# Issuing the low-half matmuls of a split-precision product after all the high-half ones

## The chip, the cores and the metric

The kernel runs on one core of a Trainium2 chip. The metric is device time of one execution in microseconds (us). The five engines of the core work from queues of their own: TensorE (matmuls, in the profile PE, with its weight loads as PEld), VectorE (DVE), ScalarE (ACT), GpSimd (POOL) and SyncE (SP, here only an issuer of transfers). They wait for one another by semaphores.

## The reference, cut to what matters

A residual stream of 16 meta tokens and 512 tokens of width 1024 goes through two layers. Layer 0 mixes by causal pooling, layer 1 by an attention over keys and values that are projected once. Each layer then has a PEER block: every token picks 8 x 16 of 16384 experts by two sets of 128 sub-keys, and adds their outputs.

```
def peer(h, w_query, sub_keys, u, v):
    q = einsum('btd,dq->btq', hx, w_query)            # query projection
    s = einsum('bthpc,hpnc->bthpn', q, sub_keys)      # scores of the sub-keys
    top_s, top_i = lax.top_k(s, 16)
    ...                                               # 256 sums, top 16, softmax -> expert, gate
    act = gelu(einsum('btd,bthkd->bthk', hx, u[expert]))
    return einsum('bthk,bthkd->btd', gate * act, v[expert])
```

## The kernel before, in words

Of the four blocks of 128 tokens three are treated densely: for each of the 128 groups of 128 experts the kernel forms gelu(u . h) for all 384 tokens (a "first product", function `u_parts`, called a step here), weighs it with a gate matrix that is zero where an expert was not picked, and multiplies by v. The experts of the fourth block (`GATHERED`) are fetched row by row with indirect transfers (`row_steps`: `prod` L354, `hx` L366 on VectorE, `row` L342 on GpSimd).

Products are of float32 values split into two halves: hi is the value rounded to the format that TensorE reads at full rate, lo is the rest. A product is hi*hi + hi*lo + lo*hi over 8 chunks of 128 in depth, 24 matmuls into one PSUM bank. In a step the weights are the stationary operand: `w_hi` (copied from the loaded `w32` by ScalarE, L278) and `w_lo` (w minus w_hi, on VectorE L280 while `gating` is set, otherwise on GpSimd L282). Both have two buffers, `w32` has three, and `load_w` of a step is called one step ahead (`following`). The moving operand is the normalised stream, `n_hi` and `n_lo`.

A PEER block has three stages. In the query stage 16 projections (two per head) and their scores alternate with steps; layer 0's projections have two PSUM tiles because of the meta tokens (L516, L517), layer 1's go through `mm3` (L123 to L125, here with weights stationary). The scores' matmuls (L530) feed VectorE's top-16 searches (`top16`, `tv`). In the gate stage `select` picks the experts on VectorE, and `build_gates` forms one-hot tiles (`hot` L612, `weighed` L616) for 8 tokens at a time, 16 such groups in each of 3 blocks, which TensorE multiplies into `pg` (L596) in groups of 16 matmuls; ScalarE copies `pg` to `stage`, which goes to memory as `gout`. Steps are cut into quarters at a `yield` (`UPARTS` = 4), and a hand-written cost account (`tu`, `td`) decides after which quarters of steps the `pg` groups stand. While `pinned` is set, TensorE's matmuls keep this order; the other queues, and TensorE's outside this stage, are ordered when the program is built, by a planner that follows program order among what its own estimate holds to be ready. In the value stage the remaining steps alternate with `v_step` (matmuls `y`, L713), whose weights `v` come straight from memory.

`mm3` is also used in the attention: for the projections to keys, queries and values (`pp` with `wn_hi`, `wn_lo`) and for its output projection (`wo_hi`, `wo_lo`). There the stream is stationary and the weights move: `whi` is `n_hi` and `wlo` is `n_lo`.

Of the kernel before, what the change touches and what calls it, by code (L numbers as in the profile page):

```python
# [22 lines left out]
KC = D // P  # L23
# [15 lines left out]
UPARTS = 4  # L39
# [19 lines left out]
def trunk_kernel(ctx: ExitStack, tc: tile.TileContext, x, meta, norm_mix, norm_ffn, pool_w, pool_scale,  # L59
                 kv_norm, w_kv, k_norm, w_q, q_norm, w_o, peer_wq, peer_keys, peer_ut, peer_uv, out):  # L60
    nc = tc.nc
    v, sc, pe, gp, sy = nc.vector, nc.scalar, nc.tensor, nc.gpsimd, nc.sync
# [58 lines left out]
    def mm3(ps, whi, wlo, xhi, xlo, kc):  # L121
        for k in range(kc):
            pe.matmul(ps, whi(k), xhi(k), start=k == 0, stop=False)  # L123
            pe.matmul(ps, whi(k), xlo(k), start=False, stop=False)  # L124
            last = pe.matmul(ps, wlo(k), xhi(k), start=False, stop=k == kc - 1)  # L125
        return last

# [126 lines left out]
    def peer(layer, with_meta, gain, hn_nat, kp, up, finish):  # L254
# [3 lines left out]
        c0 = dense[0] * P  # L258
        assert dense == list(range(dense[0], dense[0] + nd))
        ND = nd * P  # L260
# [3 lines left out]
        SM = S + NM if with_meta else S  # L264
        hi, lo = n_hi, n_lo

        with ExitStack() as cl:
# [3 lines left out]
            vmark, amark, pmark, todo = [], [], [], []  # L271
# [17 lines left out]
            def pin(x):  # L289
                return tc.keep_in_program_order(x) if pinned[0] else x  # L290
# [8 lines left out]
            def weight(key, following=None):  # L299
# [3 lines left out]
                        ahead[kk] = load_w(src[layer, kk[1]])  # L303
                return ahead.pop(key)

            def u_parts(j, spill, following=None):
                w, whi, wlo = weight(("u", j), following)
                ps = psu.tile([P, S], F32, name="psu")
                n = 0
                for k in range(KC):  # L310
                    for a, b, st, en in ((whi, hi, k == 0, False), (whi, lo, False, False),
                                         (wlo, hi, False, k == KC - 1)):
                        m = pin(pe.matmul(ps[:, :ND], a[:, k, :], b[:, k, c0:c0 + ND], start=st, stop=en))  # L313
                        n += 1
                        if n == 3 * KC:
                            pmark.append(m)
                        elif n * UPARTS % (3 * KC) == 0:
                            yield
                ac = up.tile([P, ND], F32, name="ac", bufs=FRONT + 2)
                sc.activation(ac, ps[:, :ND], AF.Gelu)  # L320
                if spill:
                    sc.dma_start(aout[j], ac)
                return ac
# [57 lines left out]
            with ExitStack() as c1:  # L381
# [92 lines left out]
                with ExitStack() as cq:  # L474
                    qp = cq.enter_context(tc.tile_pool(name="qp", bufs=1, reuse_waits="tile"))
                    keys = qp.tile([P, 2 * H, NK], F32, name="keys")
                    sy.dma_start(keys, peer_keys[layer])
                    if with_meta:
                        zq = qp.tile([P, 2 * H, H, NM], F32, name="zq")
                        psq = cq.enter_context(tc.tile_pool(name="psq", bufs=2, reuse_waits="tile", space=PSUM))  # L480
                        gp.memset(zq, 0.0)
                    plan = []
                    nu = 0
                    for _ in range(LEAD[layer]):
                        plan.append(("u", nu))
                        nu += 1
                    for h in range(H):
                        plan += [("w", 2 * h), ("w", 2 * h + 1)]
                        td += WQ_DVE[layer]
                        tu += WQ_PE[layer]  # L490
                        while tu < td and h > 0:
                            plan.append(("u", nu))
                            nu += 1
                            tu += ucost
                    plan.append(("u", nu))
                    plan.reverse()
                    while plan[-1][0] == "u":
                        u_step(plan.pop()[1], True, plan[-1])
                        j0 += 1
                    norm_split(gr, ps1, NT - 1, hx[NT - 1], gain, hn_nat[NT - 1], pt_name="ps1", junk="prod")  # L500
                    ym = kp.tile([P, D], F32, name="gain") if with_meta else None

                    for h in range(H):
                        qts = []
                        for pp in range(2):
                            hp = 2 * h + pp
                            w, whi, wlo = weight(plan.pop(), plan[-1])
                            ps = psu.tile([P, S], F32, name="psu")
                            qt = qp.tile([P, S], F32, name="qt", bufs=3)
                            if with_meta:  # L510
                                half = SM // 2
                                ps2 = psq.tile([P, half], F32, name="psq")
                                for k in range(KC):
                                    for wp, xp, st, en in ((whi, hi, k == 0, False), (whi, lo, False, False),
                                                           (wlo, hi, False, k == KC - 1)):
                                        pe.matmul(ps[:, :half], wp[:, k, :], xp[:, k, :half], start=st, stop=en)  # L516
                                        pe.matmul(ps2, wp[:, k, :], xp[:, k, half:SM], start=st, stop=en)  # L517
                                sc.activation(qt[:, :half], ps[:, :half], AF.Copy)
                                sc.activation(qt[:, half:], ps2[:, :S - half], AF.Copy)
                                sc.activation(zq[:, hp, h, :], ps2[:, S - half:], AF.Copy)  # L520
                            else:
                                mm3(ps, lambda k: whi[:, k, :], lambda k: wlo[:, k, :],
                                    lambda k: hi[:, k, :S], lambda k: lo[:, k, :S], KC)
                                sc.activation(qt, ps, AF.Copy)
                            qts.append(qt)
                        for i2 in range(0, NT, 2):
                            pss = ps1.tile([P, 2, 2, NK], F32, name="ps1")
                            for ii in range(2):
                                for pp in range(2):
                                    pe.matmul(pss[:, ii, pp, :], qts[pp][:, (i2 + ii) * P:(i2 + ii + 1) * P],  # L530
                                              keys[:, 2 * h + pp, :], start=True, stop=True)
                            s = qp.tile([P, 2, 2, NK], F32, name="s", bufs=3)
                            sc.activation(s, pss, AF.Copy)
                            for ii in range(2):
                                for pp in range(2):
                                    top16(qp, s[:, ii, pp, :], NK, tv[i2 + ii][:, h, pp, :],
                                          ti[i2 + ii][:, h, pp, :])
                        tq += 26.0 if h >= GH else 0.0
                        while len(plan) > 1 and plan[-1][0] == "u":
                            u_step(plan.pop()[1], True, plan[-1])  # L540
                            j0 += 1
                        if h % GH == GH - 1:
                            hs = slice(h - GH + 1, h + 1)
                            for i in gathered:
                                res = []
                                for _ in select(qp, gr, f"g{i}_{h}", tv[i][:, hs], ti[i][:, hs], GH, res):
                                    pass
                                gather_rows(i, h, *res, GH * TK, hx[i], False)
                        while tr < tq and row_step():
                            tr += ROW_PERIOD[layer][0] / 8  # L550
                    if with_meta:
                        pss = ps1.tile([P, 2, 2, NK], F32, name="ps1")
                        for pp in range(2):
                            for h in range(H):
                                pe.matmul(pss[:, 0, pp, :], zq[:, 2 * h + pp].rearrange("p g t -> p (g t)"),
                                          keys[:, 2 * h + pp, :], start=h == 0, stop=h == H - 1)
                        s = qp.tile([P, 2, 2, NK], F32, name="s", bufs=3)
                        sc.activation(s[:, 0], pss[:, 0], AF.Copy)
                        for pp in range(2):
                            top16(qp, s[:, 0, pp, :], NK, tvm[:, 0, pp, :], tim[:, 0, pp, :])  # L560
# [515 lines left out]
```

## Time and profile before

| | us |
|---|---|
| median of 3 runs | 3077.86 |
| lowest and highest of them | 3077.44, 3078.27 |
| the profiled execution | 3071.0 |
| its span, first to last instruction | 3069.3 |
| TensorE busy in the span | 2914.3 (95%) |
| TensorE weight loads busy | 2597.2 (85%) |
| VectorE busy | 2321.5 (76%) |
| ScalarE busy | 1313.3 (43%) |
| GpSimd busy | 664.3 (22%) |

The profile is one execution. A group of instructions is told with its busy time and the idle time of its engine just before it, by whom that wait was ended. A line of the chain of waits is a piece of the work that ended last, followed back from the end. Where an engine is named as the one waited for, its instruction was the last of several conditions to come true by the profile. Idle time of an engine that does not set the end of a stretch costs nothing.

### The profile page before, as it was taken

How to read it: one execution, taken by the hardware profiler on the slowest of the kernel's cores; microseconds unless marked ns; L12 is line 12 of the kernel's file. 1: busy time of each engine (PE TensorE's matmuls, PEld its weight loads, DVE VectorE, ACT ScalarE, POOL GpSimd, SP SyncE). 2: the span in 40 equal slices, each digit the busy share in tenths (PEclk: the TensorE clock that was granted, in tenths of full speed). 3: DMA queues.
4: the chain of work that ended last, by engine and by line, in shares of the span. 5: the costliest groups of instructions: out<-in, count | busy, mean ns of one | idle time of the engine just before them, and what ended most of it. 6: DMA issues, size and time to landing. Idle time of an engine off the chain costs nothing.

```text
span 3069.3 us, 45150 instructions
## 1 busy us (share of the span) xinstructions
PE 2914.3 (95%) x16514; PEld 2597.2 (85%) x16514; DVE 2321.5 (76%) x4807; ACT 1313.3 (43%) x2154; POOL 664.3 (22%) x702
## 2 busy tenths in 40 slices
PE   8987999999999999999999998798999999999999
PEld 7977898988888887779965787798998888888887
DVE  3699979678887878866456437999777888788875
ACT  3323646454333333344456333355546333333333
POOL 3441111111211211104235244311110211111100
PEclk9998999999999999999999999999999999999999
DMA  3266778789999999952100324677887999898985
GB/s 131 99 234 217 267 271 314 268 329 392 325 341 325 337 316 328 366 187 80 56 1 1 110 100 172 231 248 278 285 306 284 364 350 334 310 338 312 377 278 168
DMA packets 294768, 769.50 MB, mean 251 GB/s; under 512 B 24080, under 2 KB 184848, under 8 KB 256400
## 3 DMA queue, kind: packets, MB, share of 16 engines
q1 hardware_dynamic: 226576, 396.43, 38.0%
q0 software_dynamic: 39168, 285.23, 24.8%
q10 hardware_dynamic: 28800, 84.95, 7.2%
q8 instruction: 129, 2.11, 0.3%
q14 instruction: 95, 0.78, 0.1%
HBM read 679.49 MB, written 87.03 MB: 250 GB/s over the span
## 4 chain that ended last, share of the span: by engine, by line
PE 76%; DVE 15%; DMA 5%; ACT 2%; issue 2%; POOL 1%; SPq 0%; DVEq 0%; ACTq 0%; POOLq 0%
PE y L713 30%; PE psu L313 27%; DMA v<-in_peer_uv_dram 3%; PE pp L124 2%; PE pp L125 2%; PE pp L123 2%; PE pg L596 2%; DVE w_lo L280 2%; DVE prod L354 1%; PE psq L517 1%; PE psu L516 1%; DVE hx L366 1%; DVE weighed L616 1%; DVE hot L612 1%; DVE mr L394 1%
## 5 line engine op out<-in xcount | busy, mean ns | idle before, releaser
L313 PE MATMUL psu<-n_hi,w_lo 128*128 128x384 f32 x2048 | 700.2, 342 | 73.7 <-DVE w_lo L280 69.4
L342 POOL DMA_INDIRECT row<-in_peer_uv_dram,ei x272 | 363.8, 1337 | 1767.5 <-DVE hx L366 1492.2
L313 PE MATMUL psu<-n_hi,w_hi 128*128 128x384 f32 x2048 | 707.6, 346 | 4.4 <-ACT w_hi L278 3.9
L313 PE MATMUL psu<-n_lo,w_hi 128*128 128x384 f32 x2048 | 699.9, 342 | 0.6 <-DVE n_lo L118 0.6
L278 ACT ACTIVATE w_hi<-w 128x1024 fp32r<-128x1024 f32 x288 | 305.2, 1061 | 498.2 <-PE psu L313 351.0
L713 PE MATMUL y<-v_hi,wt_hi 128*128 128x512 f32 x1536 | 474.9, 390 | 6.5 <-ACT wt_hi L705 4.5
L713 PE MATMUL y<-v_lo,wt_hi 128*128 128x512 f32 x1536 | 475.8, 391 | 5.1 <-DVE v_lo L699 5.0
L713 PE MATMUL y<-v_hi,wt_lo 128*128 128x512 f32 x1536 | 474.6, 390 | 1.2 <-DVE wt_lo L706 1.2
L313 PEld LDWEIGHTS psu<-n_hi,w_lo 128*128 128x128 f32 x2048 | 391.5, 191 | 82.9 <-DVE w_lo L280 77.1
L313 PEld LDWEIGHTS psu<-n_hi,w_hi 128*128 128x128 f32 x2048 | 389.2, 190 | 9.1 <-ACT w_hi L278 5.2
L313 PEld LDWEIGHTS psu<-n_lo,w_hi 128*128 128x128 f32 x2048 | 389.9, 190 | 3.9 <-DVE n_lo L118 1.1
L705 ACT ACTIVATE wt_hi<-wt 128x384 fp32r<-128x384 f32 x256 | 134.3, 525 | 529.5 <-PE y L713 292.7
L280 DVE TENSOR_TENSOR w_lo<-w,w_hi 128x1024 fp32r<-128x1024 f32 x230 | 280.1, 1219 | 100.0 <-ACT w_hi L278 98.9
L713 PEld LDWEIGHTS y<-v_lo,wt_hi 128*128 128x128 f32 x1536 | 288.1, 188 | 69.4 <-DVE v_lo L699 10.1
L713 PEld LDWEIGHTS y<-v_hi,wt_lo 128*128 128x128 f32 x1536 | 289.0, 188 | 62.3 <-DVE wt_lo L706 2.0
L354 DVE SCALAR_TENSOR_TENSOR prod<-row,hnat 128x1024 bf16<-128x1024 f32 x272 | 337.9, 1242 | 5.0 <-DMA row<-in_peer_uv_dram,ei 4.8
L713 PEld LDWEIGHTS y<-v_hi,wt_hi 128*128 128x128 f32 x1536 | 288.0, 188 | 62.8 <-ACT wt_hi L705 5.0
L366 DVE SCALAR_TENSOR_TENSOR hx<-row,gwt,hx 128x1024 f32<-128x1024 f32 x256 | 329.6, 1287 | 2.6
L699 DVE TENSOR_TENSOR v_lo<-v,v_hi 128x1024 fp32r<-128x1024 f32 x256 | 312.1, 1219 | 20.2 <-ACT v_hi L698 20.2
L698 ACT ACTIVATE v_hi<-v 128x1024 fp32r<-128x1024 f32 x256 | 270.9, 1058 | 61.0 <-DMA v<-in_peer_uv_dram 59.3
L706 DVE TENSOR_TENSOR wt_lo<-wt,wt_hi 128x384 fp32r<-128x384 f32 x256 | 142.1, 555 | 203.2 <-ACT wt_hi L705 202.9
L601 ACT ACTIVATE stage<-pg 128x512 f32<-128x512 f32 x192 | 200.9, 1156 | 81.7 <-PE pg L596 80.9
(283 smaller groups left out, 4110.6 us busy)
## 6 DMA issues: line engine op xcount, KB each, us to landing
w<-in_peer_ut_dram SPq DMA_DIRECT2D x256, 512.0 KB, 5.2
v<-in_peer_uv_dram SPq DMA_DIRECT2D x256, 512.0 KB, 6.8
gout<-stage ACTq DMA_DIRECT2D x24, 2048.0 KB, 8.4
gt<-gout SPq DMA_DIRECT2D x64, 768.0 KB, 9.8
aout<-ac ACTq DMA_DIRECT2D x176, 192.0 KB, 3.5
ac<-aout SPq DMA_DIRECT2D x176, 192.0 KB, 7.0
w<-in_peer_wq_dram SPq DMA_DIRECT2D x32, 512.0 KB, 3.3
wn<-in_w_kv_dram SPq DMA_DIRECT2D x8, 1024.0 KB, 5.5
```

The source lines that it names most:

```text
L278: amark.append(sc.activation(whi, w, AF.Copy))
L280: vmark.append(v.tensor_sub(wlo, w, whi.bitcast(F32)))
L313: m = pin(pe.matmul(ps[:, :ND], a[:, k, :], b[:, k, c0:c0 + ND], start=st, stop=en))
L342: gp.indirect_dma_start(out=row, out_offset=None, in_=peer_uv, in_offset=bass.IndirectOffsetOnAxis(ap=item[1], axis=0))
L354: v.scalar_tensor_tensor(prod, row[:, :D], 1.0, hn_nat[i], ALU.mult, ALU.mult, accum_out=dot)
L366: v.scalar_tensor_tensor(acc, row[:, D:], wt, acc, ALU.mult, ALU.add)
L601: sc.activation(stage[:, :, o:o + 4].rearrange("p j t -> p t j"), pg, AF.Copy, scale=1.0 / GSCALE)
L698: amark.append(sc.activation(vhi, v32, AF.Copy))
L699: vmark.append(v.tensor_sub(vlo, v32, vhi.bitcast(F32)))
L705: sc.activation(whi, wt, AF.Copy)
L706: vmark.append(v.tensor_sub(wlo, wt, whi.bitcast(F32)))
L713: pe.matmul(y[n][half], wp[:, ts], vq[:, half * 512:(half + 1) * 512], start=st, stop=en)
```

## The change

For each product over 8 chunks the order of the 24 matmuls is changed. Before: for each chunk k, `w_hi[k]` with the stream's high half, `w_hi[k]` with its low half, `w_lo[k]` with its high half. After it: for all chunks the two products with `w_hi`, then for all chunks the product with `w_lo`. This holds for the steps, for layer 0's projections (each of the 24 there is a pair of matmuls), and for everything that calls `mm3`. The sums, the number of matmuls, the buffers and the places of the yields by count of matmuls stay as they are.

```diff
@@ -122,6 +122,7 @@
         for k in range(kc):
             pe.matmul(ps, whi(k), xhi(k), start=k == 0, stop=False)
             pe.matmul(ps, whi(k), xlo(k), start=False, stop=False)
+        for k in range(kc):
             last = pe.matmul(ps, wlo(k), xhi(k), start=False, stop=k == kc - 1)
         return last
@@ -303,19 +304,25 @@
+            def low_last(whi, wlo):
+
+                for k in range(KC):
+                    yield whi, hi, k, k == 0, False
+                    yield whi, lo, k, False, False
+                for k in range(KC):
+                    yield wlo, hi, k, False, k == KC - 1
+
             def u_parts(j, spill, following=None):
                 w, whi, wlo = weight(("u", j), following)
                 ps = psu.tile([P, S], F32, name="psu")
                 n = 0
-                for k in range(KC):
-                    for a, b, st, en in ((whi, hi, k == 0, False), (whi, lo, False, False),
-                                         (wlo, hi, False, k == KC - 1)):
-                        m = pin(pe.matmul(ps[:, :ND], a[:, k, :], b[:, k, c0:c0 + ND], start=st, stop=en))
-                        n += 1
-                        if n == 3 * KC:
-                            pmark.append(m)
-                        elif n * UPARTS % (3 * KC) == 0:
-                            yield
+                for a, b, k, st, en in low_last(whi, wlo):
+                    m = pin(pe.matmul(ps[:, :ND], a[:, k, :], b[:, k, c0:c0 + ND], start=st, stop=en))
+                    n += 1
+                    if n == 3 * KC:
+                        pmark.append(m)
+                    elif n * UPARTS % (3 * KC) == 0:
+                        yield
@@ -510,11 +517,9 @@
-                                for k in range(KC):
-                                    for wp, xp, st, en in ((whi, hi, k == 0, False), (whi, lo, False, False),
-                                                           (wlo, hi, False, k == KC - 1)):
-                                        pe.matmul(ps[:, :half], wp[:, k, :], xp[:, k, :half], start=st, stop=en)
-                                        pe.matmul(ps2, wp[:, k, :], xp[:, k, half:SM], start=st, stop=en)
+                                for wp, xp, k, st, en in low_last(whi, wlo):
+                                    pe.matmul(ps[:, :half], wp[:, k, :], xp[:, k, :half], start=st, stop=en)
+                                    pe.matmul(ps2, wp[:, k, :], xp[:, k, half:SM], start=st, stop=en)
```

## Rows read from the trace of the kernel before

**Rows 1.** The page: span, engines, one of its costliest groups (busy, mean ns | idle before).
```profile
span 3069.3 us, 45150 instructions
...
PE 2914.3 (95%) x16514; PEld 2597.2 (85%) x16514; DVE 2321.5 (76%) x4807; ACT 1313.3 (43%) x2154; POOL 664.3 (22%) x702
...
L313 PE MATMUL psu<-n_hi,w_lo 128*128 128x384 f32 x2048 | 700.2, 342 | 73.7 <-DVE w_lo L280 69.4
```

**Rows 2.** Busy times by stretch: us, PE, PEld, DVE, ACT, POOL, PEclk, DMA share, GB/s.
```profile
143.00:217.00 74.00, 60.07 (x445) 58.56 (x444) 69.62 (x297) 24.12 (x53) 36.29 (x20) 0.91 0.58 213
219.40:410.80 191.40, 158.30 (x1039) 152.85 (x1037) 186.14 (x598) 95.95 (x133) 32.50 (x17) 0.91 0.68 242
410.80:648.00 237.20, 231.00 (x1634) 224.11 (x1635) 190.30 (x237) 132.32 (x177) 26.33 (x19) 0.99 0.80 291
...
672.00:1186.00 514.00, 512.57 (x2463) 451.16 (x2461) 422.83 (x614) 196.67 (x330) 94.90 (x79) 1.00 0.94 340
...
1947.50:2126.30 178.80, 148.65 (x956) 142.34 (x954) 174.48 (x534) 88.70 (x124) 32.03 (x18) 0.93 0.69 248
2126.30:2362.00 235.70, 230.40 (x1612) 223.66 (x1613) 188.77 (x234) 130.21 (x173) 28.35 (x18) 0.99 0.82 292
```

**Rows 3.** TensorE's waits (us, times, longest), gate stages' halves: two of the first, then one each.
```profile
PE psu L313 <- DVE w_lo L280: 31.4, 7, 19.3
PE pg L596 <- DVE weighed L616: 1.7, 1, 1.7
...
PE psu L313 <- DVE w_lo L280: 4.8, 4, 2.3
...
PE psu L313 <- DVE w_lo L280: 27.6, 8, 9.2
...
PE psu L313 <- DVE w_lo L280: 6.5, 5, 2.3
```

**Rows 4.** VectorE's waits: layer 0's first half (two), its second, layer 1's first (two).
```profile
DVE hot L612 <- PE pg L596: 4.4, 2, 2.3
DVE w_lo L280 <- ACT w_hi L278: 0.7, 2, 0.4
...
DVE w_lo L280 <- ACT w_hi L278: 34.9, 21, 3.0
...
DVE w_lo L280 <- ACT w_hi L278: 2.6, 3, 1.5
DVE hot L612 <- PE pg L596: 1.0, 1, 1.0
```

**Rows 5.** The chain of waits (start, us, what): a value-stage step, a gate-stage step.
```profile
681.76 4.23 PE psu L313 x24
...
2174.63 4.29 PE psu L313 x24
```

**Rows 6.** The chain of waits after a wait for `w_lo`, layer 0's first half.
```profile
340.73 3.57 PE psu L313 x10
344.30 1.73 PE pg L596 x16
```

**Rows 7.** TensorE's waits from 217 to 219.4 us, at layer 0's gate entry.
```profile
PE psu L313 <- POOL w_lo L282: 2.2, 1, 2.2
```

**Rows 8.** Layer 1's query stage, 1866 to 1947 us: waits, one piece of the chain.
```profile
PE psu L125 <- POOL w_lo L282: 9.2, 2, 6.1
...
DVE tv L392 <- ACT s L533: 9.6, 1, 9.6
...
1903.30 0.23 PE psu L124
```

**Rows 9.** Groups by line: the attention's projections with the weights' low half.
```profile
L124 PE MATMUL pp<-wn_lo,n_hi 128*128 128x256 f32 x384 | 109.9, 286 | 0.0
...
L124 PE MATMUL pp<-wo_lo,n_hi 128*128 128x256 f32 x128 | 37.2, 292 | 1.7 <-DVE wo_lo L1006 1.7
```

**Rows 10.** The chain of waits at the end of layer 0's gate stage.
```profile
649.90 11.21 DMA gout<-stage
```

## The prediction

> **What bounds the kernel now.** I read the page first: one span of 3069.3 us [rows 1] in an execution of 3071.0 us, 6.9 us under the median of the three timed runs (3077.86 us); differences are formed on the profiled execution and then taken off the median. Its costliest groups show the target: the matmuls of a first product that read the low half `w_lo` stood behind 73.7 us of idle TensorE, nearly all of it waiting for VectorE's subtraction at L280 [rows 1]. That adds up stages with different limits, so the busy times by stage come next. In the value stage TensorE is busy 512.6 of 514 us: nothing can be hidden there. The gate stages have two halves. In the first half of each (219.4 to 410.8 us in layer 0, 1947.5 to 2126.3 us in layer 1) VectorE is busy 186.1 of 191.4 and 174.5 of 178.8 us, TensorE only 158.3 and 148.7; in the second half TensorE is busy 231.0 of 237.2 and 230.4 of 235.7 us and VectorE has room [rows 2]. So the first halves belong to VectorE, the second halves to TensorE.
>
> The waits say how the lost time divides. TensorE waits for `w_lo` 31.4 and 27.6 us in the first halves, but 4.8 and 6.5 us in the second [rows 3]. VectorE in turn idles in the first halves only 4.4 and 1.0 us for `pg` matmuls that free a `hot` buffer, and 0.7 and 2.6 us for a `w_hi` that waits for its own buffer; in layer 0's second half the latter is 34.9 us, which is its room [rows 4]. A wait of TensorE in a stretch that VectorE fills costs the end nothing; VectorE's own idle time there does.
>
> **The change part by part.** It adds and removes no instruction: a step has the same 24 matmuls and weight loads, 3 products for 8 chunks. It moves eight of them behind sixteen.
>
> (a) The head start. Before, `w_lo` is read by the third matmul of a step, after it by the seventeenth. A step of 24 matmuls of 384 columns takes 4.23 us [rows 5], 0.176 us each, so `w_lo` may come 14 x 0.176 = 2.46 us later before anything stands. For layer 1's projections of 512 columns a matmul takes 0.23 us [rows 8], so there it is 14 x 0.23 = 3.2 us. The quarters end after 6, 12 and 18 matmuls as before; a gate group `pg` that follows matmul 12 now stands ahead of the wait for `w_lo` and no longer behind it.
>
> (b) The early release. The last read of `w_hi` was matmul 23 and becomes matmul 16: 7 x 0.176 = 1.2 us earlier for the ScalarE copy L278 that refills it, and so for VectorE's next subtraction. `w_lo` is released at matmul 24 as before. The load of the next `w32` on SP waits for a subtraction, so no transfer is moved later on its queue, at most 1.2 us earlier.
>
> The sum, stretch by stretch:
> 1. Entry of layer 0's gate stage: TensorE stands 2.2 us for a `w_lo` from GpSimd [rows 7], in its order ahead of the score matmuls that VectorE then waits for. 2.2 is under 2.46: 2.2 us.
> 2. First half, layer 0: VectorE's idle 4.4 + 0.7 us. The chain shows its making: TensorE resumes after a `w_lo` wait, needs 3.57 us for 10 matmuls and 1.73 us for the 16 of `pg`, and only then may `hot` be built [rows 6]. With (a) that `pg` precedes the wait; with (b) the `w_hi` waits, 0.4 us at most each, go. 5.1 us.
> 3. Second half, layer 0: four waits, the longest 2.3 us, all under 2.46: 4.8 us.
> 4. First half, layer 1: VectorE's 1.0 + 2.6 us, for the same reasons: 3.6 us.
> 5. Second half, layer 1: five waits, the longest 2.3 us: 6.5 us.
> 6. Query stage, layer 1: L125 waits twice for GpSimd's `w_lo`, 6.1 and 3.1 us, and VectorE then stands 9.6 us for scores that come out of that stretch [rows 8]. Of the 6.1 us the head start takes 3.2; the 3.1 I count at nothing, because VectorE is busy when they pass (if it weren't, they would be 3.1 us more). In layer 0's query stage VectorE is busy 69.6 of the last 74 us [rows 2], so TensorE's waits there count nothing.
>
> 2.2 + 5.1 + 4.8 + 3.6 + 6.5 + 3.2 = 25.4 us.
>
> What it could cost. Pace: in the low run the weights go from one `w_lo` chunk to the next, an order that the trace does not show. The same 24 matmuls took 4.23 us in the value stage and 4.29 in a gate stage [rows 5]. I take 4.23, the row where TensorE is disturbed least; the upper end is 0.06 x 256 steps = 15 us. A gain is excluded: no matmul, column or load disappears. The projections through `mm3` in the attention are mirrored: there the weights are the moving operand, and chunk k is now needed after 2k matmuls and not 3k, at most 7 matmuls earlier, which are shorter than L313's, so under 7 x 0.176 = 1.2 us. TensorE waited 0.0 us for `wn_lo` and 1.7 us for `wo_lo` [rows 9]; I take nothing, as the cover is a conversion that ran far ahead, and 1.2 us at each of the two first groups if it is not. The end of a gate stage is a chain of transfers (`gout` for 11.21 us, then the first values [rows 10]); it starts when the last `pg` ends and moves along with it, so it gives and takes nothing.
>
> Where the stalls go: in the first halves TensorE still stands, at `w_lo` or at `pg`, because VectorE is what is late next.
>
> The Trainium skill, Perfetto Trace Analysis, Identifying the Most-Contended Engine, says that a kernel gains by relieving the engine of highest occupancy. Over the span that is TensorE, 95% against VectorE's 76% [rows 1]. By it each of the 15 waits of the first halves [rows 3] would be worth up to the head start, 15 x 2.46 = 37 us in place of the 8.7 us of items 2 and 4, and the sum would be 54 us. By stage, VectorE's 97% there speaks against it.
>
> **The rivals.**
> A. Only TensorE's half pays. VectorE's queue is planned anew, and the small idle times (items 2 and 4) and the entries (1 and 6) come back elsewhere. Then items 3 and 5 alone count, 11.3 us: 3066.6. For it: they are a few waits of 0.4 to 2.3 us, and TensorE's order in the query stages is not pinned. Against: their cause, a `w_hi` or `pg` behind a `w_lo` wait, is taken away in any order.
> B. More than the sum. With `w_hi` earlier the planner puts the subtractions earlier in VectorE's queue and leaves gather rows to the second half, where VectorE idles 34.9 us [rows 4]; part of the 59 us of first-half waits then counts. With a third of the 37 us on top of the rest it is 25.4 + 12 = 38 us: 3040. The chain also shows TensorE at half its pace after a wait, 0.357 us a matmul against 0.176 [rows 6, 5]; a shorter wait may give that back too. The Trainium skill, TensorE: Matmul & The Clock Gate, HAM oscillation, has the same rule: after idle gaps the next burst starts at half rate. The trace agrees in that row.
> C. Slower. The subtractions become ready 1.2 us earlier and the planner sets them ahead of `hot` and `weighed` in VectorE's queue; `pg` is pinned in TensorE's order, so TensorE now stands at `pg`. A subtraction costs 1.2 us, and 21 of the 96 builds of gates (3 blocks of 16 in 2 layers) would have to get one put ahead on the path to eat the 25.4 us. With 30 it is 36 - 25 = 11 us worse: 3089. For it: a wait of `pg` for `weighed` exists already, 1.7 us [rows 3]. Against: in the second halves VectorE has 34.9 us of room.
> D. No change. Each `w_lo` wait reappears whole at the next `pg`, since one VectorE queue feeds both: 3078. Against: in the second halves TensorE waits for `w_lo` and not at all for `weighed` [rows 3].
>
> **How the numbers follow.** Forecast 3077.9 - 25.4 = 3052.5 us (profiled execution about 3046), chance 0.62; its own range, with 15 us of pace on one side and half of B's extra on the other, is 3046 to 3068. A 0.16, B 0.07, C 0.08, D 0.07. The range is 3037 to 3074: it takes in A and B and leaves out C and D, 0.15. 0.2% is 6.2 us, about what a measurement can tell. Faster by more than that: forecast, A and B, less what A loses to the pace, 0.82; within: D and that part of A, 0.10; slower: C, 0.08.
>
> **What would show it.** The row of L313 with `w_lo` should fall from 73.7 us of idle time to under 40, what remains lying in the first halves behind long VectorE stretches, and none in the second halves. VectorE busy over 98% in the first halves, which shorten by some 5 us from 191 and by 4 from 179 us. The value stage unchanged at 24 matmuls in 4.23 us. Wrong would be: steps of 4.29 us in the value stage, new waits at `pg` of the size of the old ones at `w_lo`, or first halves as long as before.

## The result, and the profile after

The changed kernel takes 3024.61 us (median of 4 runs, 3016.17 to 3028.53) against 3077.65 us (3073.45 to 3078.27) for the kernel before, measured beside it: a ratio of 0.9824, 95% interval 0.9806 to 0.9842. That is 53 us less, where 25.4 were forecast; the time lies below the range.

The page of after: span, engines, and the group that answers to the last of [rows 1].
```profile
span 3014.5 us, 45155 instructions
...
PE 2892.9 (96%) x16514; PEld 2581.2 (86%) x16514; DVE 2313.7 (77%) x4807; ACT 1332.1 (44%) x2154; POOL 704.4 (23%) x702
...
L320 PE MATMUL psu<-n_hi,w_lo 128*128 128x384 f32 x2048 | 411.9, 341 | 34.3 <-DVE w_lo L281 34.3
```
The idle time in front of the `w_lo` matmuls falls from 73.7 to 34.3 us. (Their busy time falls only because neighbours of one group now overlap in the records; the mean of one is 341 ns against 342.) TensorE's busy and idle time give the plainest account: before it is busy 2914.3 of 3069.3 us, so idle 155.0; after it is busy 2892.9 and idle 121.6. The span is 54.8 us shorter: 33.4 us of idle time and 21.4 us of busy time, with the same 16514 matmuls. These accounts are of one execution each: the changed kernel's is the fastest of its four, the kernel before's (3071.0 us) lies below all four of its own, and that of three runs (below) is the slowest of its four.

To see where, I cut both traces at the same instructions: the last scores of a layer, the first `pg` matmul of its blocks, the last `pg`. A stretch then holds the same matmuls in both kernels, within five. Busy times by stretch as in [rows 2], before, both gate stages:
```profile
219.50:314.30 94.80, 74.28 (x422) 73.15 (x420) 94.80 (x400) 34.48 (x55) 16.90 (x10) 0.89 0.62 215
314.30:455.90 141.60, 129.01 (x872) 124.56 (x871) 122.06 (x241) 76.59 (x104) 20.93 (x11) 0.95 0.77 277
455.90:648.20 192.30, 186.10 (x1382) 179.35 (x1381) 159.54 (x194) 117.36 (x152) 21.10 (x15) 0.99 0.80 291
...
1947.60:2031.50 83.90, 66.29 (x351) 64.51 (x349) 83.64 (x341) 28.32 (x46) 15.43 (x11) 0.92 0.66 231
2031.50:2173.50 142.00, 129.47 (x872) 124.80 (x871) 121.68 (x236) 76.42 (x103) 22.12 (x11) 0.96 0.75 270
2173.50:2365.70 192.20, 186.90 (x1382) 180.13 (x1381) 159.53 (x193) 117.53 (x154) 22.73 (x14) 0.99 0.81 292
```
The same stretches after:
```profile
216.90:310.10 93.20, 74.94 (x427) 73.47 (x426) 91.91 (x369) 35.87 (x55) 12.58 (x10) 0.91 0.66 234
310.10:442.00 131.90, 126.01 (x873) 122.25 (x872) 124.04 (x272) 77.54 (x103) 25.23 (x11) 0.99 0.83 296
442.00:628.60 186.60, 183.85 (x1381) 178.11 (x1381) 158.47 (x194) 118.78 (x153) 31.22 (x15) 1.00 0.82 300
...
1908.00:1988.20 80.20, 65.74 (x356) 64.84 (x355) 80.06 (x313) 29.63 (x47) 13.39 (x9) 0.91 0.66 228
1988.20:2118.70 130.50, 124.61 (x873) 120.63 (x873) 120.22 (x255) 78.30 (x104) 22.54 (x11) 1.00 0.83 295
2118.70:2302.70 184.00, 183.76 (x1381) 178.61 (x1381) 162.64 (x205) 118.15 (x152) 32.64 (x14) 1.00 0.85 303
```
The second line of each layer, from the first `pg` of block 0 to the first of block 1, carries most: 141.6 to 131.9 and 142.0 to 130.5 us. Before, neither engine fills it: VectorE is busy 122 us, TensorE 129 at a granted clock of 0.95. After, TensorE is busy 126 of 131.9 and 124.6 of 130.5 at 0.99 and 1.00. In the first two lines of both layers together TensorE's idle time falls by some 19 us and its busy time by some 8.

The whole span by such cuts, beside the items of the prediction's sum (us):

| stretch | before | after | change | forecast |
|---|---|---|---|---|
| start to last scores, layer 0 | 219.5 | 216.9 | -2.6 | item 1: -2.2 |
| to block 1's first `pg` | 236.4 | 225.1 | -11.3 | item 2: -5.1 |
| to last `pg`, layer 0 | 192.3 | 186.6 | -5.7 | item 3: -4.8 |
| value stage, attention, to first scores of layer 1 | 1141.3 | 1134.5 | -6.8 | 0 |
| query stage, layer 1, first to last scores | 158.1 | 144.9 | -13.2 | item 6: -3.2 |
| to block 1's first `pg` | 225.9 | 210.7 | -15.2 | item 4: -3.6 |
| to last `pg`, layer 1 | 192.2 | 184.0 | -8.2 | item 5: -6.5 |
| value stage, layer 1, to the end | 703.6 | 711.8 | +8.2 | 0 |

The waits in layer 0's stretch of block 0 to block 1, before (314.3 to 455.9 us):
```profile
PE psu L313 <- DVE w_lo L280: 10.9, 4, 5.5
...
DVE w_lo L280 <- ACT w_hi L278: 14.0, 10, 3.0
```
The same stretch, parted where the prediction parted it, and VectorE's wait in the second part:
```profile
314.30:410.80 96.50, 83.91 (x617) 79.60 (x616) 91.30 (x199) 61.43 (x79) 15.50 (x7) 0.93 0.75 269
410.80:455.90 45.10, 45.10 (x256) 44.96 (x256) 30.76 (x43) 15.16 (x25) 5.43 (x4) 1.00 0.82 292
...
DVE w_lo L280 <- ACT w_hi L278: 13.2, 8, 3.0
```
And after (310.1 to 442.0 us):
```profile
PE pg L601 <- DVE weighed L621: 3.0, 5, 1.1
PE ps L576 <- DVE gdi L460: 2.6, 1, 2.6
...
DVE w_lo L281 <- ACT ga L365: 4.0, 2, 2.2
DVE w_lo L281 <- PE psu L320: 1.6, 1, 1.6
DVE w_lo L281 <- ACT w_hi L279: 0.4, 1, 0.4
```
Before, the two engines stand in turn: TensorE stands for `w_lo`, and a little later, while TensorE catches up without a gap, VectorE stands for a `w_hi` that TensorE has not released. After, both waits are all but gone; TensorE's small ones for gate tiles are left, and 6.0 us of VectorE's at the same subtraction.

### The profile page after: what moved, and what is told of

The parts are those of the page before. It is cut to its first block, busy times and chain, and to the rows that moved or that the text cites. A ratio compares the mean times of both kernels' runs of the same rounds, so it can differ in the third digit from the quotient of the medians.

```text
span 3014.5 us, 45155 instructions
## 1 busy us (share of the span) xinstructions
PE 2892.9 (96%) x16514; PEld 2581.2 (86%) x16514; DVE 2313.7 (77%) x4807; ACT 1332.1 (44%) x2154; POOL 704.4 (23%) x702
## 4 chain that ended last, share of the span: by engine, by line
PE 75%; DVE 14%; DMA 7%; ACT 2%; issue 2%; POOL 0%; SPq 0%; DVEq 0%; ACTq 0%; POOLq 0%
PE y L718 28%; PE psu L320 28%; DMA v<-in_peer_uv_dram 3%; PE pg L601 2%; PE pp L126 2%; PE pp L124 2%; PE pp L123 2%; DMA ac<-aout 1%; DVE prod L361 1%; DVE hx L373 1%; PE psq L522 1%; PE psu L521 1%; DVE w_lo L281 1%; DVE mr L401 1%; DVE hot L617 1%
## 5 line engine op out<-in xcount | busy, mean ns | idle before, releaser
L349 POOL DMA_INDIRECT row<-in_peer_uv_dram,ei x272 | 404.3, 1487 | 1675.1 <-DVE hx L373 1379.7
L320 PE MATMUL psu<-n_hi,w_hi 128*128 128x384 f32 x2048 | 698.9, 341 | 2.8 <-ACT w_hi L279 1.9
L320 PE MATMUL psu<-n_lo,w_hi 128*128 128x384 f32 x2048 | 692.1, 338 | 0.6 <-DVE n_lo L118 0.6
L320 PE MATMUL psu<-n_hi,w_lo 128*128 128x384 f32 x2048 | 411.9, 341 | 34.3 <-DVE w_lo L281 34.3
L320 PEld LDWEIGHTS psu<-n_hi,w_lo 128*128 128x128 f32 x2048 | 362.3, 190 | 36.6 <-DVE w_lo L281 36.5
L704 DVE TENSOR_TENSOR v_lo<-v,v_hi 128x1024 fp32r<-128x1024 f32 x256 | 312.3, 1220 | 18.7 <-ACT v_hi L703 18.7
```

The costliest lines, as they stand in the source:

```text
L349: gp.indirect_dma_start(out=row, out_offset=None, in_=peer_uv, in_offset=bass.IndirectOffsetOnAxis(ap=item[1], axis=0))
L704: vmark.append(v.tensor_sub(vlo, v32, vhi.bitcast(F32)))
```

## The experiments

Twelve kernels were run, each beside the kernel before. Their traces give TensorE's account (us; the profiled execution) and the length of both gate stages together, last scores to last `pg`:

| kernel | median | ratio, 95% interval | span | TensorE busy | idle | gate stages |
|---|---|---|---|---|---|---|
| before | 3077.65 | | 3069.3 | 2914.3 | 155.0 | 846.8 |
| after | 3024.61 | 0.9806 to 0.9842 | 3014.5 | 2892.9 | 121.6 | 806.4 |
| steps only | 3032.87 | 0.9838 to 0.9874 | 3030.1 | 2898.6 | 131.5 | 805.9 |
| projections only | 3070.47 | 0.996 to 0.9991 | 3063.5 | 2910.3 | 153.2 | 847.4 |
| head start only | 3044.43 | 0.9857 to 0.9901 | 3044.0 | 2903.3 | 140.7 | 815.4 |
| early release only | 3049.47 | 0.9887 to 0.9934 | 3044.2 | 2897.8 | 146.4 | 823.5 |
| three runs | 3023.93 | 0.9775 to 0.9838 | 3031.1 | 2901.6 | 129.5 | 806.3 |

**Which part carries it.** The steps changed alone (the kernel before with the diff's part in `u_parts`), and `mm3` and layer 0's projections changed alone.
```diff
-                for k in range(KC):
-                    for a, b, st, en in ((whi, hi, k == 0, False), (whi, lo, False, False),
-                                         (wlo, hi, False, k == KC - 1)):
+                for a, b, k, st, en in low_last(whi, wlo):
```
```diff
         for k in range(kc):
             pe.matmul(ps, whi(k), xhi(k), start=k == 0, stop=False)
             pe.matmul(ps, whi(k), xlo(k), start=False, stop=False)
+        for k in range(kc):
             last = pe.matmul(ps, wlo(k), xhi(k), start=False, stop=k == kc - 1)
```
Steps only, expected: 

> Only the steps (first products) issue their low run last; the projections of both layers and mm3 keep the old order. Theory: the gate stages gave 17 and 24 us of the 54.8 us, the query stage of layer 1 another 13, and that one comes from mm3; so this kernel gains some 38 to 42 us, 3036 to 3040 us, with layer 1's query stage (first to last score matmul, 158 us before, 145 after) back at 158. Rival: the query stage's 13 us come from the steps that stand between the projections there; then this gains all of it, about 3025 us.

Projections only, expected: 

> Only the projections and mm3 have the new order, the steps the old one. Theory: 13 us from layer 1's query stage and nothing elsewhere, 3062 to 3067 us, gate stages as long as before (429 and 418 us). Rival (the query stage gains by its steps): no change, 3075 to 3080 us.

Measured: ratio 0.9856 for the steps and 0.9975 for the projections, some 44 and 8 us, which add up to the whole. With the steps alone the gate stages are 40.9 us shorter, as in the changed kernel (40.4); with the projections alone they keep their length, and layer 1's query stage is 151.1 us long instead of 158.1 (155.7 with the steps alone). In that stage the waits for GpSimd's `w_lo` [rows 8] are gone; TensorE's wait for the copy `qt`, 1.1 us before, is 8.5 us in these lines of its trace, 1788 to 1942 us:
```profile
PE ps L542 <- ACT qt L536: 8.5, 3, 6.0
DVE tv L406 <- ACT s L545: 50.5, 5, 20.2
```

**Not VectorE's new order.** In the order of VectorE's queue, 32 MAX8 instructions (16 top-16 searches over candidates, two instructions to a search) stand between block 0's last reduction `gdi` and block 1's before the change, and none between block 1's and block 2's. After it they are 21 and 11 in layer 0, 19 and 13 in layer 1. Two kernels hold the searches of a dense block behind the `gdi` of the block before, 16 and 16, one built on the kernel before, one on the changed one.
```diff
+                        with tc.issue_after(gmark[-1].ins) if tag == "gd" and gmark else nullcontext():
                             top16(tmp, cand[:, h, :], NCAND, bv[:, h * TK:(h + 1) * TK],
                                   bp[:, h * TK:(h + 1) * TK])
...
+                        if tag == "gd" and half == 1:
+                            gmark.append(red)
```
On the kernel before, expected: 

> The kernel before, with one thing added: VectorE's top-16 searches over the candidates of a dense block are issued only after the index sums (gdi) of the block before. In the queue of before, all 32 first searches of blocks 1 and 2 lie between block 0's sums and block 1's; here 16 and 16, as in none of the two kernels so far (21 and 11 after the change). Theory that the new queue order of VectorE carries the part of the gain that the prediction missed: some 10 us of VectorE's work leave the first half of each gate stage, so 15 to 20 us faster, 3058 to 3063 us, without any change on TensorE. Rival (the gain is the head start and the early release themselves, the queue order follows but carries nothing): 3075 to 3080 us, as VectorE's work only changes places.

On the changed one, expected: 

> The changed kernel with the same hold on the searches: 16 and 16 in place of 21 and 11 (layer 0) and 19 and 13 (layer 1). Theory: 5 and 3 more search groups of about 0.7 us leave the first halves, 4 to 7 us faster than the changed kernel, 3017 to 3021 us. Rival: no difference to the changed kernel, 3025 us, because TensorE's work now sets the first halves too.

Measured: 3075.38 us, ratio 0.9998 (0.9982 to 1.0013), and 3026.16 us, ratio 0.9833 (0.9811 to 0.9854). An evener queue gains nothing by itself, and the gain does not hang on the queue that the planner happened to choose.

**Head start against early release.** Two orders of a step's 24 matmuls, in the steps alone. The first reads `w_lo` from matmul 15 on but keeps the last chunk of `w_hi` to the end; the second still reads one chunk of `w_lo` as its third matmul and releases `w_hi` early.
```diff
+                for k in range(KC - 1):
+                    yield whi, hi, k, k == 0, False
+                    yield whi, lo, k, False, False
+                for k in range(KC):
+                    yield wlo, hi, k, False, False
+                yield whi, hi, KC - 1, False, False
+                yield whi, lo, KC - 1, False, True
```
```diff
+                for k in range(KC):
+                    yield whi, hi, k, k == 0, False
+                    yield whi, lo, k, False, False
+                    if k == 0:
+                        yield wlo, hi, k, False, False
+                for k in range(1, KC):
+                    yield wlo, hi, k, False, k == KC - 1
```
Head start only, expected: 

> Steps only; w_lo is first read by matmul 15 instead of 3, but the last chunk of w_hi is read by the last two matmuls, so w_hi is not released earlier than before. Theory head start (it carries the gain of the steps, since TensorE stands for w_lo in both gate stages and the early release moves only copies that nobody waits for): the two gate stages are 17 and 23 us shorter, as with the steps' whole change, and the time is 3033 to 3040 us. Rival early release (w_hi, its copy and the subtraction behind it come 1.2 us earlier, and VectorE's queue flows better): the gate stages lose no more than 10 us together, and the time is 3065 us or more.

Early release only, expected: 

> Steps only; w_hi is last read by matmul 17 as in the change's step less one, but the first chunk of w_lo is still read by the third matmul, so there is no head start. Theory head start: the gate stages shorten by at most 8 us together and the time is 3068 to 3078 us. Rival early release: the gate stages shorten by over 25 us together and the time is under 3050 us. If both halves are needed, each alone gives clearly less than the 45 us of the two together.

Measured: 3044.43 and 3049.47 us, ratios 0.9879 and 0.9911, some 37 and 27 us by the ratios; the gate stages are 31.4 and 23.3 us shorter, with both halves 40.9. Neither theory holds alone. The head start brings most but ends 4 us above its range, the early release brings 23.3 us where it was given at most 8, and the two together bring less than their sum. The waits over the whole span, of the kernel before, head start only, early release only, and steps only:
```profile
PE psu L313 <- DVE w_lo L280: 69.4, 23, 19.3
DVE w_lo L280 <- ACT w_hi L278: 98.9, 62, 7.5
```
```profile
PE psu L321 <- DVE w_lo L280: 45.6, 11, 17.5
DVE w_lo L280 <- ACT w_hi L278: 95.7, 67, 6.8
```
```profile
PE psu L321 <- DVE w_lo L280: 53.1, 16, 18.7
DVE w_lo L280 <- ACT w_hi L278: 29.6, 20, 8.3
```
```profile
PE psu L319 <- DVE w_lo L280: 35.7, 8, 17.2
DVE w_lo L280 <- ACT w_hi L278: 18.2, 10, 8.3
```
The head start leaves VectorE's waits for `w_hi` as they were and takes 24 us off TensorE's waits for `w_lo`. The early release takes 69 us off VectorE's waits for `w_hi`, and TensorE's for `w_lo` fall by 16 us with them, though `w_lo` is still read by the third matmul. But more than half of that is a change of name: with the early release the same subtraction stands 37.0 us for TensorE to free a `w_lo` buffer, a wait that the kernel before does not have:
```profile
DVE w_lo L280 <- PE psu L321: 37.0, 16, 3.0
```
Whatever they wait for, VectorE's gaps in front of these subtractions come to 100.0 us before, 97.5 with the head start, 73.2 with the early release, 60.2 with the steps alone. I read this as a ring in which the two engines stand: TensorE's last read of `w_hi`, ScalarE's copy, VectorE's subtraction, TensorE's first read of `w_lo`. Slack on either side of it would loosen the same ring, and so the halves would not add; that the two gains come about in this way is argued and not shown. Both orders also run a step of the value stage in 4.18 us instead of 4.23 (under "Pace"); if the gate stages' 154 steps run faster by as much, an estimate, some 7 us of the 31.4 and of the 23.3 are pace and no wait.

**The ring by another means.** A third `w_hi` buffer gives the copy a whole step of slack without any new order; it fits only with two buffers of `w32` in place of three, so that kernel is its measure.
```diff
-W32 = 3
+W32 = 2
-                whi = up.tile([P, KC, P], F32R, name="w_hi", bufs=2)
+                whi = up.tile([P, KC, P], F32R, name="w_hi", bufs=3)
```
Third `w_hi`, expected: 

> The kernel before with its order of matmuls, with three buffers for w_hi instead of two, and two for w32 instead of three to make room. The copy into w_hi then waits for the step before last, 4.2 us earlier than now, as an early release without any change of order. Theory (the ring of TensorE's last read of w_hi, ScalarE's copy, VectorE's subtraction and TensorE's next step is what the early release loosens): VectorE's waits for w_hi fall well below their 98.9 us, and against the kernel with two w32 alone the gate stages shorten by about the 23 us that the early release gave. Rival (the order of the matmuls or the new queue order gave it): no gain against the kernel with two w32 alone.

Two `w32` alone, expected: 

> The kernel before with two buffers for w32 instead of three, as the measure for the kernel that also has a third w_hi. A load of w is then issued one step later. If the loads are not what is late, within 6 us of the kernel before; if they are, slower, with waits for the transfer of w.

Measured: 3104.09 us, ratio 1.009 (1.0061 to 1.0119), and 3094.48 us, ratio 1.0048 (1.0033 to 1.0062). The waits of the kernel with the third `w_hi`:
```profile
ACT w_hi L278 <- DMA w<-in_peer_ut_dram: 387.4, 135, 14.2
...
PE pg L596 <- ACT stage L601: 15.0, 18, 4.0
```
The copy now waits for the transfer of `w` and, being first in ScalarE's queue, holds back the copies of `pg` to `stage` behind it; TensorE stands 15.0 us for them. VectorE's waits for `w_hi` did fall, from 118.4 us with two `w32` to 62.8 (some 19 of these 56 us came back as waits for TensorE to free `w_lo`), and TensorE's for `w_lo` from 70.6 to 51.1, as the ring would have it, but the time does not show it. This test of the ring settled nothing.

**Pace.** The changed kernel with the 16 high matmuls cut into two runs, so that no two neighbours share a weight.
```diff
                 for k in range(KC):
                     yield whi, hi, k, k == 0, False
+                for k in range(KC):
                     yield whi, lo, k, False, False
```
Expected: 

> The changed kernel with the 16 high matmuls of a product cut again: first all chunks of w_hi with the stream's high half, then all with its low half, then the low run (steps and layer 0's projections). The head start and the release stay within one matmul; the weights now differ from each matmul to the next. Theory (the step's 4.19 us instead of 4.23 in the value stage come from the place of the weights in the order, but are no large part of the gain): 24 matmuls in the value stage take 4.15 to 4.30 us and the time is within 8 us of the changed kernel's 3024.6. Rival (pace is what was gained): the step goes back to 4.23 us or more and the gate stages lose over 10 us of their gain.

Measured: 3023.93 us, the changed kernel's time. Steps in the value stage by the chain of waits, after and with three runs (start, us, what):
```profile
2602.97 4.19 PE psu L320 x24
```
```profile
2754.39 4.21 PE psu L321 x24
```
The step took 4.23 us before [rows 5] and takes 4.19 after; the two halves alone give 4.18. So the order of the weights is worth a little, 0.02 to 0.05 us a step, and the gain does not hang on it: with 4.21 the time is the same as with 4.19.

**Does TensorE's wait count where VectorE is gapless?** Between the last scores and the first `pg` VectorE is busy 91.9 of 93.2 and 80.1 of 80.2 us after the change, while TensorE waits 18.3 and 14.5 us. Two kernels keep the gathered rows out of that stretch, and differ in when the rows are made up for; a third takes the subtractions there off VectorE.
```diff
-ROW_PERIOD = ((18.0, 23.0, 13.5), (18.0, 23.0, 13.5))
+ROW_PERIOD = ((18.0, 18.0, 13.5), (18.0, 18.0, 13.5))
...
+                    if blocks[0] == nd * (P // TG):
+                        tr = td
                     while tr < td and blocks[0] >= QUIET and row_step():
```
```diff
+                    if blocks[0] == nd * (P // TG):
+                        tr = td
                     while tr < td and blocks[0] >= QUIET and row_step():
-                        tr += ROW_PERIOD[layer][1] / 8
+                        tr += (ROW_PERIOD[layer][1] if blocks[0] > 2 * (P // TG) else 17.0) / 8
```
```diff
-                pinned[0] = gating[0] = True
+                pinned[0] = True
...
                         for cost in build_gates(n, *res):
+                            gating[0] = True
                             blocks[0] -= 1
```
Rows held, expected: 

> The changed kernel, but the gathered rows (prod and hx, some 2.5 us of VectorE each) are kept out of the stretch between a gate stage's last scores and its first gate tiles, and their period in the rest of the stage is 18 instead of 23. In that stretch VectorE is busy 91.9 of 93.2 and 80.1 of 80.2 us, 22 and 19 us of it with rows, and TensorE stands 18.3 and 14.5 us. Theory (VectorE alone sets that stretch; TensorE's waits there cost nothing by themselves): it shortens by 18 to 22 us in layer 0 and 15 to 19 us in layer 1, the next stretch grows by up to 8 us each, and the time is 2995 to 3012 us. Rival (the rows only come back later, in stretches that VectorE also limits, or at the end): the stage keeps its length within 5 us and the time is 3018 us or more.

Rows later, expected: 

> The changed kernel, with the gathered rows again kept out of the stretch between the last scores and the first gate tiles; their period stays 23 in the first third of the gate tiles, as in the changed kernel, and is 17 only after that, where VectorE idles 24 and 16 us. Theory now (TensorE's account: the steps are the same wherever they stand, so only TensorE's waits and its slow matmuls count; the stretch gets 20 us shorter, but by as many matmuls that have to be done later, and TensorE's 17 us of waits there stay): within 8 us of the changed kernel's 3024.6 us. Rival (what the prediction held: VectorE's own work sets that stretch, and taking 14 us of rows out of it in each layer is a gain): 2995 to 3012 us.

Measured: 3037.6 us, ratio 0.9867 (0.9842 to 0.9893), and 3027.97 us, ratio 0.9837 (0.982 to 0.9853). The stretch does what VectorE's work says, and yet nothing is gained. Busy times of the two stretches with the rows later, and TensorE's waits in the first:
```profile
220.00:292.50 72.50, 54.82 (x313) 54.24 (x312) 72.48 (x343) 27.41 (x39) 6.81 (x5) 0.88 0.52 185
1914.40:1977.10 62.70, 49.80 (x260) 48.63 (x260) 62.51 (x255) 22.96 (x34) 7.53 (x5) 0.89 0.52 180
```
```profile
PE psu L320 <- DVE w_lo L281: 16.3, 1, 16.3
```
The stretch is 20.7 us shorter in layer 0, but 114 matmuls fewer are done in it (313 against 427), 20 us at 0.176 us each, and those have to be done later. TensorE's waits there, 16.3 and 1.4 us, stay as they were, and so does the time of the kernel. The shorter period of the rows moves more than that: both gate stages together are 58 us longer than in the changed kernel and hold 306 matmuls more, and the stretches behind them are 55 us shorter. So steps can stand anywhere, and a shorter stretch is no gain by itself. That TensorE's waits there would pay if they went was not shown, as neither kernel takes them away. Rows held costs 13 us more than the changed kernel, and 10 more than rows later; against rows later it loses 13.6 us between layer 0's last `pg` and layer 1's first scores (1124.4 against 1110.8 us, the same matmuls within one, 9.7 us more of idle TensorE). Why is open.

Low half on GpSimd, expected: 

> The changed kernel, but until the first gate tiles of a layer are built the subtractions that make w_lo are on GpSimd (2.4 us each there) and not on VectorE (1.2 us). In that stretch VectorE is gapless and TensorE stands 18.3 and 14.5 us for w_lo. Theory (a wait of TensorE in a stretch that VectorE fills costs the end nothing, only VectorE's own work counts): the stretch shortens by the 7 to 10 subtractions of 1.2 us taken off VectorE, 8 to 12 us in each layer, and the time is 3005 to 3012 us, if GpSimd delivers in time. Rival (TensorE's wait counts there too): it shortens by 15 to 18 us in each layer, and the time is under 3000 us. Rival (GpSimd, which issues the row transfers, is late, or its work slows VectorE's): no gain, 3020 us or more.

Measured: 3047.42 us, ratio 0.9898 (0.988 to 0.9917), 23 us slower than the changed kernel. Three of VectorE's groups from 216 to 330 us, after:
```profile
L399 DVE MAX8 bv<-cand 128x8 f32<-128x80 f32 x17 | 3.7, 232 | 0.0
...
L455 DVE TENSOR_TENSOR hot<-hot,tib 128x2048 f16<-128x2048 f16 x2 | 2.4, 1220 | 0.0
L414 DVE TENSOR_TENSOR cand<-tv 128x128 f32<-128x128 f32 x7 | 1.8, 279 | 0.0
```
and with the low half on GpSimd, with GpSimd's own group in that stretch of layer 0:
```profile
L414 DVE TENSOR_TENSOR cand<-tv 128x128 f32<-128x128 f32 x10 | 12.1, 1205 | 0.0
...
L399 DVE MAX8 bv<-cand 128x8 f32<-128x80 f32 x22 | 4.8, 228 | 0.0
L455 DVE TENSOR_TENSOR hot<-hot,tib 128x2048 f16<-128x2048 f16 x2 | 4.6, 2302 | 0.0
```
```profile
L283 POOL TENSOR_TENSOR w_lo<-w,w_hi 128x1024 fp32r<-128x1024 f32 x16 | 40.6, 2543 | 18.0 <-ACT w_hi L279 9.6 <-PE psu L320 8.2
```
VectorE's additions into `cand` take 1205 ns on average instead of 279, the operation on `hot` 2302 instead of 1220, the searches the same; the stretch grows from 93.2 to 108.5 us. TensorE still stands there, 12.6 us behind ScalarE's `ac` and 3.3 us for `w_lo`, so this kernel does not tell what those waits cost.

## Why the prediction was wrong

The direction, the place (mostly the gate stages) and the row to watch were right: 73.7 us of idle time before `w_lo` matmuls were to fall under 40 with none left in the second halves, and 34.3 are left, all in the stretches before block 1's first `pg`. The size forecast was half of what came.

**The step that failed** is the sentence "A wait of TensorE in a stretch that VectorE fills costs the end nothing", with the cut on which it rested. The cut at 410.8 us parted what belongs together: the 96 us in which VectorE is late, and the 45 us after them in which TensorE catches up and VectorE waits for `w_hi`. Taken as one piece, 314.3 to 455.9 us, VectorE idles 19.5 of 141.6 us, so the piece could shrink until one of the engines has no gap. I had counted 34.9 us of VectorE's waits for `w_hi` [rows 4] as its room; 13.2 of them lie in these 45 us and go with TensorE's waits. TensorE's 10.9 us of waits for `w_lo` in the piece fell to nothing, and the piece by 9.7 us. Of the 31.4 and 27.6 us of first-half waits [rows 3], then, the part in these pieces paid. The rest lies before the first `pg`, where VectorE has no gap (94.8 of 94.8 us); there the change took away little (TensorE idle 20.5 us before, 18.3 after, and 17.6 and 14.5 in layer 1). That VectorE sets even that stretch is not borne out by the rows moved later, which made it shorter and gained nothing; whether TensorE's waits in it cost the end stays open.

By the items of the sum:
- Items 1, 3 and 5, the waits of TensorE taken at full, were near: 2.2, 4.8 and 6.5 us against 2.6, 5.7 and 8.2.
- Items 2 and 4, priced by VectorE's small waits, are the miss: 5.1 and 3.6 us against 11.3 and 15.2. The early release (b), put at 1.2 us for a copy that hardly anyone waits for, takes 23.3 us off the gate stages when it stands alone, pace included.
- Item 6 had the right two waits, but the second, 3.1 us, was counted at nothing. In the seven kernels with the projections changed, rows held and rows later among them, the query stage is 6 to 13 us shorter, not 3.2 (158.1 us before; 144.9 in the changed kernel's profiled execution, 146.5 to 152.0 in the others), and 2.4 us of it come with the steps alone. What its 512-column matmuls at half pace cost, counted one by one, was 4 us before and is nothing in these seven.
- "A gain is excluded" of the pace was wrong twice. The engine's busy time fell by 21.4 us: the step takes 4.19 us instead of 4.23, which over 256 steps is 10 us at most (in the value stage the 36 `y` matmuls between two steps take 8.18 us instead of 8.16, so half of what a step gains there is given back); and what matmuls at half pace after a wait [rows 6] cost, counted one by one, falls by some 8 us in the gate stages and some 4 in layer 1's query stage, which the granted clock of 0.95 and 0.96 going to 0.99 and 1.00 in the stretches above shows too. The forecast named this in rival B and left it out of the sum.
- Nothing was put on the value stages. Layer 1's takes 8.2 us longer, 7.0 of them idle TensorE. At its start the chain of waits has a load of `w` of 15.54 us behind `gout` and a load of `v`, where before it had `gout` and a load of `v` alone. With the steps alone layer 1's gate stage is followed by 707.0 us, with three runs by 713.0, before by 703.6. Why is not settled.

Of the rivals C (slower) and D (nothing) are out, and A (11.3 us) with them. B had the direction, more than the sum, and the clock, but its mechanism, subtractions and rows ordered anew by the planner, is not the cause. Held searches change the time of neither kernel, and the rows and subtractions did not change their stretches: `prod` of the gathered rows stands 9, 11 and 14 times in layer 0's three stretches and 8, 11 and 14 times in layer 1's, before and after, and the subtractions differ by one. The rule weighed in the prediction, of the Trainium skill, Perfetto Trace Analysis, Identifying the Most-Contended Engine, gave 54 us, an estimate, by taking TensorE over the whole span; measured are 53. The total agrees and its parts do not, so there is luck in it: of TensorE's 54.8 us only 33.4 are idle time, and the stretches of items 2 and 4 gave 26.5, not 37 us. The 97% of VectorE [rows 2] that I set against it was a share of half a period.

As forecast, no new waits of the old size stand at `pg` (7.6 us in all for `weighed`). Not as forecast, VectorE does not fill the first halves: 124.0 of 131.9 and 120.2 of 130.5 us from block 0's first `pg` to block 1's, where over 98% was expected of the halves.

## What to carry to other kernels

Where two engines wait for each other in turn, cut the trace at the same instruction of one full period of the work, and ask what both could lose; a share of busy time over half a period makes one of them look like the bound. If the work of the engine that is busiest over the span can be put anywhere, a stretch that gets shorter is no gain as long as that engine's idle time stays the same: count its idle time over the span. In a product of several terms, read the operand that comes last at the end and be done early with the one that is refilled first: alone they were worth some 37 and 27 us here, both 44, a small gain in pace included.

## What the runs showed of the hardware that was not expected

A subtraction of two tensors on GpSimd (2.5 us) can stop a VectorE instruction that reads two tensors. In the run with the low half on GpSimd five additions into `cand` overlap a subtraction: three last 1768, 4518 and 5320 ns, two 276 and 278, and the 27 others of the same stretches 273 on average; the searches' MAX8 on `cand`, which reads one tensor, lasts 227 with an overlap and 226 without. The Trainium skill, SBUF — State Buffer, SBUF: two separate sides, says that GpSimd and a VectorE instruction with two inputs in that memory lock each other out for a whole instruction, whichever starts first; the trace agrees in the three long ones.

The same 24 matmuls took 4.23, 4.21, 4.19 or 4.18 us by their order alone, with all waits away; which of the changes of operand costs this was not tried further.
